# Strassen-like weight sums made by GpSimd in a tile, one addition moved ahead, preparation spread: a streaming encoder layer on one Trainium2 core

## The chip, the cores and the metric

The kernel runs on one core of one Trainium2 chip. The metric is the device time of one execution in microseconds; the median of three runs is compared. Engines are named as in the profile: PE (TensorE), DVE (VectorE), ACT (ScalarE), POOL (GpSimd), SP (SyncE, whose queue issues most of the DMAs).

## The reference

One layer of a streaming encoder on 2048 prompt tokens and 64 sample tokens, all in float32. The part that matters here is the gated MLP at the end of the layer:

```python
h2 = rmsnorm(x, g2) * (1 + sc2) + sh2
up = h2 @ w_up                                   # (T, 1024) @ (1024, 2 * 2816)
upp = jnp.concatenate([conv_buf.astype(up.dtype), up], 1)
conv = b_conv + sum(w_conv[j] * upp[:, j:j + T] for j in range(CONV_W))     # causal, width 3
a, g = jnp.split(conv, 2, -1)
x = x + gt2 * ((jax.nn.silu(g) * a) @ w_down)    # (T, 2816) @ (2816, 1024)
```

Before it come a normalisation, one input projection, a pooling mixer and an mLSTM with four heads, and an output projection; after it a final normalisation. None of these is touched.

## The kernel before, in words

The first 800 us are the attention-like half of the layer, in four groups of tokens. Then the MLP runs over three groups of 704 tokens (o.g = 0, 1, 2). Every float32 operand is split into a high and a low half, and a product is made of three passes (high x high, high x low, low x high). The split of a weight unit is made on the way: a DMA loads the raw weights, ACT copies them to the high half (L385), DVE subtracts to get the low half (L388). `pump` loads ahead and splits; up to six split units are held at a time.

The up projection takes two rows of 128 outputs at a time, row f of `a` and row f of `g`, with two halves of 352 tokens each, as a 2x2 block product of seven products instead of eight. One such unit is a *Pair*. Its products, each of 12 matmuls of 352 columns (L1547), run in this order: B11, B21, T4 of the pair before, T2, T3, B22, T1. The sums of activations (T1 to T4) are made for a whole group ahead of time (`prepare`, `sums_of`, `reload`), the sums of up weights (`wsum`, and split ones in `wsplit`) in the first half of the kernel. Results are in PSUM banks: b1 takes B11, then T2 and T1 on top; b4 takes B21 and is then started afresh by B22; b3 takes T3, and T4 on top. The values are put together on DVE: `ea` (first half-row of `a`, L1609) is B21 in b4 plus a copy `s1` of B11; `eg` (L1555) and the second halves add copies `u2` and `u4` to banks. Then come the convolution: a scale on ACT (L1530) and two taps on DVE (L1535), for `ta` and `tg`, a silu on ACT (L1656), and the gate on DVE. Since these steps lag behind, `Pair.products` weaves those of the old pair in between the products of the new one with `rest(...)`.

The rows f go in parts: 0-4, 5-9, 10-15, 16-21 in groups 0 and 1; 0-5, 6-9, 10-13, 14-17, 18-21 in group 2. After each part the down projection of these rows runs (L2043) and its result is added to x (L2060). In group 2 four of the five down projections are also done by seven products instead of eight (`Quad`, `quad_down`, L1796). They need four sums of down weights for each quad, S1 to S4, held in DRAM in `dsum`. `down_sums` makes these during groups 0 and 1: a copy from DRAM to DRAM by SP's queue (L1778), then an accumulating DMA by POOL's queue (L1781), eight such steps for each of 16 blocks.

Work that is not urgent is kept in six lists of generators (`bg`), and `tick(i)` takes one step of list i at fixed places in the program. List 0 has the final normalisation of the group before, list 1 `prepare` for the next group and then `reload`, list 5 `down_sums`. PE, DVE, ACT and POOL run in the order in which the program is written; SP's order is made by a scheduler, except where `keep_in_program_order` pins a DMA.

Of the kernel before, what the change touches and what calls it, by code (L numbers as in the profile page):

```python
# [9 lines left out]
F32 = mybir.dt.float32  # L10
F32R = mybir.dt.float32r
AF = mybir.ActivationFunctionType
ALU = mybir.AluOpType
# [3 lines left out]
P = 128  # L17
# [17 lines left out]
NP = 8  # L35
S3D, S1D, S2D, S4D = range(4)
EPS = 1e-6
# [26 lines left out]
def tile_layer(ctx: ExitStack, tc: tile.TileContext, xT, vecs, cst, rst, rowv, w_mod, w_ada, w_qkou, w_v, w_pool,  # L64
# [248 lines left out]

    dsum = dr.tile([4, P, 4, NP * P], F32, tag="dsum", name="dsum")

    def quad_units(m, j):

        c = slice(j * 256, j * 256 + 256)
        return [(w_down[2 * m, :, j * 512:(j + 1) * 512], 512), (dsum[m][:, S3D:S1D + 1, c], 512),
                (dsum[m][:, S2D:S4D + 1, c], 512), (w_quad[3, m, :, c], 256)]  # L320

# [1220 lines left out]
    def product(ps, Bo, nm, first):  # L1542
        pump()
        U = get_unit()
        for kc in range(4):
            for pi, (a, b) in enumerate(PASSES):
                pe.matmul(ps[:, :FH], U[:, a, kc * P:(kc + 1) * P], Bo.at(nm, kc, b),  # L1547
                          start=(first and kc == 0 and pi == 0), stop=(kc == 3 and pi == 2), skip_group_check=not first)
            if kc % 2:
                tick(0)  # L1550
        live[0] -= 1

# [7 lines left out]
    class Pair:  # L1560
# [10 lines left out]
        def products(self, old):  # L1571
# [23 lines left out]
            product(b2, Bo, "B21", True)  # L1595
            tick(5)
            rest((old, Pair.scale_a), (older, Pair.split_lo))
            extra(1)
            if old:
                old.last_product()  # L1600
            rest((old, Pair.taps_a), (old, Pair.sum_g0))
            extra(2)
# [3 lines left out]
            rest((old, Pair.scale_g))  # L1606
            self.ea = ext_tile(o, f, "a")
            for (a, b, d) in spans(o, 0):
                dve.tensor_tensor(out=self.ea[:, d:d + b - a], in0=b2[:, a:b], in1=self.s1[:, a:b], op=ALU.add)  # L1609
            self.b3 = mm_ps()  # L1610
# [3 lines left out]
            extra(4)  # L1614
            tick(1)
            product(self.b4, Bo, "B22", True)
            rest((old, Pair.silu))
            extra(5)
            tick(5)
            product(b1, Bo, "T1", False)  # L1620
            tick(5)

# [148 lines left out]
    def down_sums():  # L1771

        for j in range(NP // 2):
            c = slice(j * 256, j * 256 + 256)
            for s, start, more in ((S1D, 2, 3), (S3D, 0, 2), (S2D, S1D, 0), (S4D, S2D, 1)):
                for m in range(4):
                    src = w_quad[start, m, :, c] if s < S2D else dsum[m][:, start, c]
                    tc.keep_in_program_order(nc.sync.dma_start(out=dsum[m][:, s, c], in_=src))  # L1778
                    yield
                for m in range(4):  # L1780
                    pool.dma_start(out=dsum[m][:, s, c], in_=w_quad[more, m, :, c], accum_op=ALU.add)  # L1781
                    yield

    def quad_down(o, j, two, Y, first, midway):

        for m in range(4):
# [4 lines left out]
            def product(ps, u, i, nm, start, on=False):  # L1791
                U = W.at(u)
                for k, quad in enumerate(two):
                    w = (2 * k + i) * P if u == 0 else k * P if u == 3 else (2 * i + k) * P
                    for pi, (x, z) in enumerate(PASSES):
                        pe.matmul(ps, U[:, x, w:w + P], quad.d[nm][z], start=(start and k == 0 and pi == 0),  # L1796
                                  stop=(k == 1 and pi == 2), skip_group_check=not start)
# [160 lines left out]
    bg[5].append(down_sums())  # L1958
    for o in fgroups:
        Bo = B[o.g]  # L1960
        quads, more, held = {}, [], []
        Y = None
        for pi, (f0, f1_) in enumerate(SPARTS if o.g in SGS else PARTS):
# [74 lines left out]
            def down(ps, W, ks, secs, stays=False):  # L2038
                for k in ks:
# [8 lines left out]
                    if todo:  # L2048
                        do()
                    else:  # L2050
                        tick(1 - k % 2)

# [143 lines left out]
```

## Time and profile before

| | before |
|---|---|
| time, median of 3 runs | 2205.1 us (2204.74 to 2205.94) |
| profiled execution, time | 2210.41 us |
| its span, first to last instruction | 2208.6 us |
| mean granted TensorE clock | 0.998 |
| PE busy | 2176.4 us (99%), 13708 matmuls |
| DVE busy | 1626.1 us (74%) |
| ACT busy | 1037.4 us (47%) |
| POOL busy | 276.9 us (13%) |

A row of a group says what an instruction writes and reads by the names in the program, then how many there are, their busy time together and the mean of one, then how long the engine stood idle just before them and for whom. A row in order of time begins with its start and its duration in us; in brackets stand the idle time before it and who ended it. The ends of matmuls are modelled: a 352-column matmul is shown with 321 ns, though the next one starts before that.

### The profile page before, as it was taken

To read this page: it belongs to the slowest core of one execution; us is meant where nothing else is said; L and a number is where in the kernel's file an instruction comes from. 1 tells how busy PE (TensorE), PEld (TensorE's weight loads), DVE (VectorE), ACT (ScalarE), POOL (GpSimd) and SP (SyncE) were. 2 spreads that over 40 slices of the span, in tenths; PEclk is the share of its full clock that TensorE was granted. 3 is DMA by queue.
4 is the path that set the end of the run, shared out by engine and by line. 5 is a ranking of instruction groups with operands and counts; after the bars stand their busy time and mean duration, and the time that the engine had idled before them with its cause. 6 is when DMAs were issued, how large, how long until landed. Compare 5 with 4: busy or idle time off the path is not lost. (4 is left out here: it accounts for less than half of the span.)

```text
span 2208.6 us, 38414 instructions
## 1 busy us (share of the span) xinstructions
PE 2176.4 (99%) x13708; PEld 2064.1 (93%) x13708; DVE 1626.1 (74%) x2996; ACT 1037.4 (47%) x2023; POOL 276.9 (13%) x546
## 2 busy tenths in 40 slices
PE   8999999999999999999999999999999999999998
PEld 7888888888899999999999999999999999999998
DVE  4887659577765768786958677776757597888894
ACT  3653335234243446464626444545435356554554
POOL 0010001001000101010202220101101321121122
PEclk9999999999999999999999999999999999999999
DMA  9978987997898687677858977767569665555552
GB/s 345 358 249 258 333 282 236 326 322 245 291 324 270 214 298 239 224 232 239 236 166 239 308 234 222 222 213 204 176 180 270 194 200 174 162 156 178 156 195 81
DMA packets 304192, 521.68 MB, mean 236 GB/s; under 512 B 27480, under 2 KB 131288, under 8 KB 304000
## 3 DMA queue, kind: packets, MB, share of 16 engines
q1 hardware_dynamic: 283008, 482.74, 66.8%
q10 hardware_dynamic: 11776, 28.09, 3.4%
q0 software_dynamic: 9216, 8.39, 3.1%
q8 instruction: 108, 1.77, 0.3%
q14 instruction: 84, 0.69, 0.1%
HBM read 408.36 MB, written 127.52 MB: 243 GB/s over the span
## 5 line engine op out<-in xcount | busy, mean ns | idle before, releaser
L1547 PE MATMUL mm<-hx,wt 128*128 128x352 f32 x5544 | 889.6, 321 | 10.0 <-DVE ea L1609 8.0
L1547 PEld LDWEIGHTS mm<-hx,wt 128*128 128x128 f32 x5544 | 879.5, 188 | 15.0 <-ACT wt L385 9.4
L442 PE MATMUL mm<-hl,wt 128*128 128x512 f32 (+2 forms) x1920 | 395.8, 358 | 1.4 <-DMA wt<-hl_kept 1.3
L2043 PE MATMUL mm<-av,wt 128*128 128x352 f32 (+2 forms) x2400 | 385.6, 321 | 1.6 <-ACT av L1682 0.9
L385 ACT ACTIVATE wt<-raw 128x512 fp32r<-128x512 f32 (+3 forms) x510 | 288.7, 579 | 205.5 <-PE mm L2043 64.6
L2043 PEld LDWEIGHTS mm<-av,wt 128*128 128x128 f32 x2400 | 380.7, 188 | 3.9 <-ACT av L1682 1.2
L388 DVE TENSOR_TENSOR wt<-raw,wt 128x512 fp32r<-128x512 f32 (+3 forms) x510 | 323.3, 648 | 73.6 <-ACT wt L385 71.3
L442 PEld LDWEIGHTS mm<-hl,wt 128*128 128x128 f32 x1920 | 312.7, 188 | 49.0 <-issue 2.8
L442 PE MATMUL mm<-mx,wt 128*128 128x512 f32 (+1 forms) x960 | 187.0, 354 | 0.3
L442 PEld LDWEIGHTS mm<-mx,wt 128*128 128x128 f32 x960 | 158.8, 188 | 25.8 <-ACT mx L1403 1.1
L385 ACT ACTIVATE wt<-wt 128x512 fp32r<-128x512 f32 x176 | 110.4, 628 | 123.8 <-DMA wt<-wsum 105.3
L388 DVE TENSOR_TENSOR wt<-wt 128x512 fp32r<-128x512 f32 x176 | 122.2, 694 | 58.9 <-ACT wt L385 58.5
L1535 DVE SCALAR_TENSOR_TENSOR tg<-eg,V,tg 128x704 f32<-128x704 f32 (+1 forms) x132 | 125.7, 952 | 40.9 <-ACT tg L1530 38.4
L2060 DVE SCALAR_TENSOR_TENSOR x<-mm,MOD,x 128x352 f32<-128x352 f32 (+4 forms) x152 | 78.0, 560 | 82.6 <-PE mm L2043 82.6
L1535 DVE SCALAR_TENSOR_TENSOR ta<-ea,V,ta 128x704 f32<-128x704 f32 (+1 forms) x132 | 125.7, 953 | 8.5 <-ACT ta L1530 5.9
L1796 PE MATMUL mm<-av,wt 128*128 128x352 f32 x576 | 94.4, 321 | 0.0
L1796 PEld LDWEIGHTS mm<-av,wt 128*128 128x128 f32 x576 | 91.8, 188 | 0.0
L207 DVE SCALAR_TENSOR_TENSOR acc<-raw,CA,acc 128x512 f32<-128x512 f32 x84 | 60.6, 748 | 30.8 <-DMA raw<-w_ada 30.7
L1656 ACT ACTIVATE tg<-tg 128x704 f32<-128x704 f32 (+1 forms) x66 | 52.3, 793 | 62.6 <-DVE tg L1535 62.6
L1555 DVE TENSOR_TENSOR eg<-mm,u 128x352 f32<-128x352 f32 x154 | 70.2, 468 | 14.8 <-ACT u L1625 10.1
L1605 ACT ACTIVATE u<-mm 128x352 f32<-128x352 f32 x66 | 30.3, 459 | 100.7 <-PE mm L1547 66.8
L1139 PE MATMUL mm<-wt,hl 128*128 128x256 f32 (+1 forms) x576 | 70.9, 282 | 0.0
(327 smaller groups left out, 2296.9 us busy)
## 6 DMA issues: line engine op xcount, KB each, us to landing
wt<-hl_kept SPq DMA_DIRECT2D x108, 512.0 KB, 5.9
raw<-w_up SPq DMA_DIRECT2D x198, 256.0 KB, 3.9
wt<-wsum SPq DMA_DIRECT2D x176, 256.0 KB, 4.8
wt<-wsplit SPq DMA_DIRECT2D x88, 512.0 KB, 4.8
w<-w_up SPq DMA_DIRECT2D x88, 256.0 KB, 5.4
wsum<-w SPq DMA_DIRECT2D x44, 512.0 KB, 6.2
wsplit<-wt SPq DMA_DIRECT2D x44, 512.0 KB, 4.4
raw<-w_down SPq DMA_DIRECT2D x88, 256.0 KB, 3.9
```

Source lines behind the costliest of these rows:

```text
L207: dve.scalar_tensor_tensor(out=acc[s], in0=w, scalar=CA[:, k, s:s + 1], in1=acc[s], op0=ALU.mult, op1=ALU.add)
L385: act.activation(u.w[:, 0, :u.n], u.raw[:, :u.n], AF.Copy)
L388: dve.tensor_tensor(out=u.w[:, 1, :u.n], in0=u.raw[:, :u.n], in1=u.w[:, 0, :u.n].bitcast(F32), op=ALU.subtract)
L442: pe.matmul(ps[bi][:, :hi - lo], U[:, a, k % 4 * P:(k % 4 + 1) * P], mv[k][:, b, lo:hi], start=(at == 0 and pi == 0), stop=(k == order[-1] ...
L1139: pe.matmul(ps[ti][:n, :cols], h[4 * kh + k4][:, b, lo:lo + n], U[:, a, k4 % 2 * cols:(k4 % 2 + 1) * cols], start=(kh == 0 and k4 == 0 and ...
L1535: dve.scalar_tensor_tensor(out=t[:, :E], in0=ext[:, j:j + E], scalar=wc(j, f), in1=t[:, :E], op0=ALU.mult, op1=ALU.add)
L1547: pe.matmul(ps[:, :FH], U[:, a, kc * P:(kc + 1) * P], Bo.at(nm, kc, b), start=(first and kc == 0 and pi == 0), stop=(kc == 3 and pi == 2), ...
L1555: dve.tensor_tensor(out=ext[:, d:d + b - a], in0=ps[:, a:b], in1=u[:, a:b], op=ALU.add)
L1656: act.activation(self.tg[:, :E], self.tg[:, :E], AF.Silu)
L1796: pe.matmul(ps, U[:, x, w:w + P], quad.d[nm][z], start=(start and k == 0 and pi == 0), stop=(k == 1 and pi == 2), skip_group_check=not start)
L2043: pe.matmul(ps[i][:, :hi - lo], U[:, a, k % 4 * P:(k % 4 + 1) * P], av[k](b, lo, hi), start=(k == 0 and (a, b) == PASSES[0]), stop=(k == n ...
L2060: dve.scalar_tensor_tensor(out=x3[n][:, a:b], in0=ps[i][:, a - lo:b - lo], scalar=gt2(n, s), in1=x3[n][:, a:b], op0=ALU.mult, op1=ALU.add)
```

## The change

It does three things.

First, in `Pair.products` the addition that makes the first half of `ea` is issued right after the taps of the old pair's `ta`, ahead of the old pair's `eg` addition (`sum_g0`), the quad steps of slot 2 and the product T2; before it stood behind all of these.

Second, `down_sums` now loads the four 128x128 blocks of a unit into a tile `dq` (256 KB, 32 units), makes the four sums with four additions on POOL in place, and stores the tile to `dsum` (256 KB). The layouts of `dsum` and `w_quad` in DRAM change so that a unit is contiguous in each partition, and `quad_units` and `quad_down` index them accordingly. List 5 must be empty before group 2.

Third, the places of the ticks: list 5 gets one after every product (seven in a pair) instead of three in a pair, and half of those in the down projections of groups 0 and 1; list 1 gets a second one in each pair from f = 5 on in these groups, and a quarter of those in the down projections instead of half.

```diff
-    dsum = dr.tile([4, P, 4, NP * P], F32, tag="dsum", name="dsum")
+    dsum = dr.tile([4, P, NP, 2, 2 * P], F32, tag="dsum", name="dsum")
     def quad_units(m, j):
-        c = slice(j * 256, j * 256 + 256)
-        return [(w_down[2 * m, :, j * 512:(j + 1) * 512], 512), (dsum[m][:, S3D:S1D + 1, c], 512),
-                (dsum[m][:, S2D:S4D + 1, c], 512), (w_quad[3, m, :, c], 256)]
+        k = slice(2 * j, 2 * j + 2)
+        return [(w_down[2 * m, :, j * 512:(j + 1) * 512], 512), (dsum[m][:, k, 1], 512), (dsum[m][:, k, 0], 512),
+                (w_quad[m, :, k, 3], 256)]
...
     def product(ps, Bo, nm, first):
...
+        tick(5)
         live[0] -= 1
...
             product(b2, Bo, "B21", True)
-            tick(5)
             rest((old, Pair.scale_a), (older, Pair.split_lo))
...
-            rest((old, Pair.taps_a), (old, Pair.sum_g0))
+            rest((old, Pair.taps_a))
+            self.ea = ext_tile(o, f, "a")
+            for (a, b, d) in spans(o, 0):
+                dve.tensor_tensor(out=self.ea[:, d:d + b - a], in0=b2[:, a:b], in1=self.s1[:, a:b], op=ALU.add)
+            rest((old, Pair.sum_g0))
             extra(2)
             product(b1, Bo, "T2", False)
             self.u2 = half_tile("u2")
             act.activation(self.u2, b1[:, :FH], AF.Copy)
             rest((old, Pair.scale_g))
-            self.ea = ext_tile(o, f, "a")
-            for (a, b, d) in spans(o, 0):
-                dve.tensor_tensor(out=self.ea[:, d:d + b - a], in0=b2[:, a:b], in1=self.s1[:, a:b], op=ALU.add)
...
             tick(1)
+            if not o.last and f >= PARTS[0][1]:
+                tick(1)
             product(self.b4, Bo, "B22", True)
             rest((old, Pair.silu))
             extra(5)
-            tick(5)
             product(b1, Bo, "T1", False)
-            tick(5)
...
     def down_sums():
-        for j in range(NP // 2):
-            c = slice(j * 256, j * 256 + 256)
-            for s, start, more in ((S1D, 2, 3), (S3D, 0, 2), (S2D, S1D, 0), (S4D, S2D, 1)):
-                for m in range(4):
-                    src = w_quad[start, m, :, c] if s < S2D else dsum[m][:, start, c]
-                    tc.keep_in_program_order(nc.sync.dma_start(out=dsum[m][:, s, c], in_=src))
+        for j in range(NP):
+            for m in range(4):
+                q = f1.tile([P, 4, P], F32, tag="dq", name="dq")
+                tc.keep_in_program_order(nc.sync.dma_start(out=q, in_=w_quad[m, :, j]))
+                for _ in range(4):
                     yield
-                for m in range(4):
-                    pool.dma_start(out=dsum[m][:, s, c], in_=w_quad[more, m, :, c], accum_op=ALU.add)
+                a11, a12, a21, a22 = (q[:, i] for i in range(4))
+                pool.tensor_tensor(out=a22, in0=a21, in1=a22, op=ALU.add)
+                pool.tensor_tensor(out=a21, in0=a11, in1=a21, op=ALU.add)
+                yield
+                pool.tensor_tensor(out=a11, in0=a22, in1=a11, op=ALU.add)
+                pool.tensor_tensor(out=a12, in0=a11, in1=a12, op=ALU.add)
+                yield
+                yield
+                tc.keep_in_program_order(nc.sync.dma_start(out=dsum[m][:, j], in_=q.rearrange("p (a b) c -> p a (b c)", a=2)))
+                for _ in range(3):
                     yield
...
     for o in fgroups:
+        if o.g in SGS:
+            drain(5)
...
                     if todo:
                         do()
+                    elif o.last:
+                        tick(1 - k % 2)
                     else:
-                        tick(1 - k % 2)
+                        tick((1, 5, 0, 5)[k % 4])
```

DVE in the third pair of group 1, before; `ta` and `tg` are the convolutions of the old pair, L388 makes the low half of a weight unit (here B22's), L1893 is the final normalisation of group 0:

```order
L1535 SCALAR_TENSOR_TENSOR ta_14315<-ea_14199,V_105,ta_14315 128x704 x2
L1555 TENSOR_TENSOR eg_14288<-mm_14202,u2_14194 128x352
L388 TENSOR_TENSOR wt_14273<-wt_14273 128x512
L1893 SCALAR_TENSOR_TENSOR x4_9283<-x4_9283,V_105,rb_14052 128x352 x2
L1609 TENSOR_TENSOR ea_14361<-mm_14268,s1_14292 128x352
L1535 SCALAR_TENSOR_TENSOR tg_14359<-eg_14288,V_105,tg_14359 128x704 x2
```

The same place in the changed kernel, in which the lines have moved by a few (L1603 is `ea`, L387 the low half, L1900 the final normalisation):

```order
L1534 SCALAR_TENSOR_TENSOR ta_14405<-ea_14266,V_105,ta_14405 128x704 x2
L1603 TENSOR_TENSOR ea_14428<-mm_14359,s1_14383 128x352
L1555 TENSOR_TENSOR eg_14379<-mm_14293,u2_14288 128x352
L387 TENSOR_TENSOR wt_14364<-wt_14364 128x512
L1900 SCALAR_TENSOR_TENSOR x4_9288<-x4_9288,V_105,rb_14141 128x352 x2
L1534 SCALAR_TENSOR_TENSOR tg_14454<-eg_14379,V_105,tg_14454 128x704 x2
```

The addition of `ea` has gone past `eg`, the low half of B22's weights and two steps of the final normalisation; the rest stands as it did.

POOL in the first pairs of group 0, before; `ea`, `eg` and `UC` are the copies of the two columns that a group hands to the next:

```order
L1513 COPY ea<-UC 128x2
L1781 DMA dsum<-w_quad 128x256 x2
L1513 COPY eg<-UC 128x2
L1781 DMA dsum<-w_quad 128x256
L1527 COPY UC<-ea 128x2
L1527 COPY UC<-eg 128x2
```

The same engine there in the changed kernel:

```order
L1512 COPY eg<-UC 128x2
L1780 TENSOR_TENSOR dq<-dq 128x128
L1781 TENSOR_TENSOR dq<-dq 128x128
L1526 COPY UC<-ea 128x2
L1783 TENSOR_TENSOR dq<-dq 128x128
L1784 TENSOR_TENSOR dq<-dq 128x128
L1512 COPY ea<-UC 128x2
L1526 COPY UC<-eg 128x2
```

Where POOL issued DMAs between its small copies, it now makes additions in its own tile, two at a time, and the copy behind them waits for them.

SP at the start of group 0 in the changed kernel, from the load of the first tile `dq` to that of the second:

```order
L1776 DMA dq<-w_quad 128x512
L616 DMA x2d<-scr 128x576
L1869 DMA x_8978<-x2d 128x704 x2
L1869 DMA x_9131<-x2d 128x704
L376 DMA wt<-wsum 128x512
...
L1787 DMA dsum<-dq 128x512
L392 DMA wsplit<-wt 128x1024
L1869 DMA x_9288<-x2d 128x704 x2
L1869 DMA x_9456<-x2d 128x704
L392 DMA wsplit<-wt 128x1024
L376 DMA wt<-wsum 128x512
L1776 DMA dq<-w_quad 128x512
```

The store and the next load of the one tile stand in the same queue as the weight loads (`wt<-wsum`, L376), where before there were copies from DRAM to DRAM.

More of the change, by code (lines that the diff above doesn't have):

```diff
@@ L35 @@
 NP = 8
-S3D, S1D, S2D, S4D = range(4)
 EPS = 1e-6
@@ L1793, in product @@
                 for k, quad in enumerate(two):
-                    w = (2 * k + i) * P if u == 0 else k * P if u == 3 else (2 * i + k) * P
+                    w = k * P if u == 3 else (2 * k + i) * P
                     for pi, (x, z) in enumerate(PASSES):
@@ L2168 @@
         "w_quad": blocks(i["w_down"][0], NF)[:, :, :2 * NP * P].reshape(4, 2, P, NP, 2, P).transpose(
-            1, 4, 0, 2, 3, 5).reshape(4, 4, P, NP * P),
+            0, 2, 3, 1, 4, 5).reshape(4, P, NP, 4, P),
         "st_C": np.concatenate([i["state_mlstm_C"][0, 0].transpose(2, 0, 1),
```

## Prediction

> **What bounds the kernel now.** I read the page first, then who PE waited for, then the order of time on DVE, ACT and SP at each place where PE stood.
>
> ```profile
> span 2208.6 us, 38414 instructions
> PE 2176.4 (99%) x13708; PEld 2064.1 (93%) x13708; DVE 1626.1 (74%) x2996; ACT 1037.4 (47%) x2023; POOL 276.9 (13%) x546
> PEclk9999999999999999999999999999999999999999
> ...
> PE mm L1547 <- DVE ea L1609: 8.0, 10, 1.3
> PE mm L1547 <- ACT wt L385: 1.1, 2, 0.6
> PE mm L2043 <- ACT av L1682: 0.9, 1, 0.9
> ...
> 1826.52 23.75 PE mm L1796 x150
> ```
>
> PE is busy for 99% of the span at full clock, and the change leaves its 13708 matmuls as they are, so only idle time of PE can be won. It is 32.2 us in all, most of it before the first matmul and after the last. From 800 us on, the waits of PE (line: total in us, times, longest) have one large entry: ten waits for the addition `ea` on DVE, L1609. The chain's row gives the beat, 23.75 / 150 = 158 ns for a 352-column matmul. The groups model a matmul's end at 321 ns, so each listed wait is 0.16 us shorter than what PE really lost: 8.0 + 10 x 0.16 = 9.6 us. That is the stock this change can draw on.
>
> Why PE waits there: the product B22 starts afresh in the bank from which `ea` reads B21, so it cannot start before `ea` has read it. DVE works in order, and `ea` stands behind other work. Three places, one of each kind (start, us, what, idle before and its releaser), the first in group 1:
>
> ```profile
> 1304.96 1.94 DVE L1535 SCALAR_TENSOR_TENSOR ta<-ea,V,ta 128x704 f32<-128x704 f32 x2
> 1306.81 0.52 DVE L1555 TENSOR_TENSOR eg<-mm,u 128x352 f32<-128x352 f32 x1
> 1307.25 0.68 DVE L388 TENSOR_TENSOR wt<-wt 128x512 fp32r<-128x512 f32 x1
> 1307.85 1.08 DVE L1893 SCALAR_TENSOR_TENSOR x<-x,V,rb 128x352 f32<-128x352 f32 x2
> 1308.84 0.52 DVE L1609 TENSOR_TENSOR ea<-mm,s 128x352 f32<-128x352 f32 x1
> ...
> 1303.71 4.91 PE L1547 MATMUL mm<-hx,wt 128*128 128x352 f32 x30
> 1309.51 1.19 PE L1547 MATMUL mm<-hx,wt 128*128 128x352 f32 x6 [0.88 <-DVE ea L1609]
> ```
>
> PE restarts 0.15 us after `ea` ends (1309.36 to 1309.51); without it B22 would have begun at about 1308.5.
>
> ```profile
> 1050.53 1.94 DVE L1535 SCALAR_TENSOR_TENSOR ta<-ea,V,ta 128x704 f32<-128x704 f32 x2 [0.24 <-ACT ta L1530]
> 1052.39 0.52 DVE L1555 TENSOR_TENSOR eg<-mm,u 128x352 f32<-128x352 f32 x1
> 1052.82 0.68 DVE L388 TENSOR_TENSOR wt<-wt 128x512 fp32r<-128x512 f32 x1
> 1053.42 0.52 DVE L1609 TENSOR_TENSOR ea<-mm,s 128x352 f32<-128x352 f32 x1
> 1054.09 1.22 PE L1547 MATMUL mm<-hx,wt 128*128 128x352 f32 x6 [0.96 <-DVE ea L1609]
> ...
> 1024.33 1.17 ACT L385 ACTIVATE wt<-wt 128x512 fp32r<-128x512 f32 x2 [4.25 <-DMA wt<-wsum]
> 1024.99 0.69 DVE L388 TENSOR_TENSOR wt<-wt 128x512 fp32r<-128x512 f32 x1 [5.58 <-ACT wt L385]
> 1025.60 0.52 DVE L1609 TENSOR_TENSOR ea<-mm,s 128x352 f32<-128x352 f32 x1
> 1026.26 1.99 PE L1547 MATMUL mm<-hx,wt 128*128 128x352 f32 x11 [0.98 <-DVE ea L1609]
> ...
> SPq L843 <- DMA Bd<-fscr: 5.5, 3, 2.6
> ...
> 1936.21 0.96 DVE L1703 TENSOR_TENSOR fscr<-ta,tg 128x640 f32<-128x640 f32 x2 [0.86 <-ACT tg L1656]
> 1938.79 1.40 PE L1547 MATMUL mm<-hx,wt 128*128 128x352 f32 x7 [0.71 <-DVE ea L1609]
> ```
>
> **Part one, `ea` ahead of the old pair's `eg`.** No instruction is added. `ea` moves ahead of the old row's addition L1555, of the quad steps of slot 2, of the subtraction L388 that makes the low half of B22's own weights, and of what the ticks of T2 put in (here L1893). What stays in the way is that L388: B22's third matmul needs the low half, and it now stands 0.44 us later (the step from L1555 to L388 in the rows above). So each wait becomes the later of two ends.
>
> First kind, more than these stood ahead of `ea`: at 1308 L388 would end at 1307.93 + 0.44 = 1308.4, in time, and all of 0.88 + 0.16 is won. At 1938 `ea` slips into the 0.86 us in which DVE waits for the silu on ACT. Four of the ten are of this kind (1309.5, 1791.1, 1938.8, 2019.7); taking off what L388 still holds back in three of them I take 3.5 us of their 3.9. Second kind, nothing but L1555 and L388 stood between (1054.1, 1549.6, 2100.1, 2142.5): DVE finishes both at the same moment as before, only in another order, and B22 gains the two matmuls that run before the low half is needed, 2 x 0.158 = 0.32 us; four of them 1.3 us. Third kind, a late load holds L388 itself (1026.3, 1495.8): PE starts at the weights' end, 1025.68, rather than behind `ea`, and the third matmul runs at 1025.8 where it ran at 1026.6; 0.8 us each, 1.6. Four shorter stops (841, 1776, 1858, 2127), listed under ACT or too short to be listed, also end 0.15 us after an `ea`; by the same reading 1.5 us. Sum 7.9 us won, with ends 4.5 (fourteen places of the second kind, 14 x 0.32) and 11 (the 9.6 and those 1.5, all of it).
>
> What is late next: the old `eg` starts 0.44 us later where DVE is behind, and with it the copy `u` on ACT, which waits for `eg` to have read the old one, and the weight splits queued behind that copy. `u` is wanted by T1, two products after T2; B22's 12 x 158 ns = 1.9 us cover it. I take nothing; without the cover 0.44 us at some of the fourteen places.
>
> **Part two, the sums for the down product made on POOL.** It takes out 64 additions by DMA from POOL's queue and 64 copies from SP's, and adds 32 loads and 32 stores of 256 KB on SP and 128 additions of 128x128 on POOL.
>
> ```profile
> L1781 POOL DMA_DIRECT2D dsum<-w_quad x64 | 53.3, 897 | 13.9 <-issue 11.4 <-DMA wsplit<-wt 1.1 <-DMA dsum<-w_quad 0.8
> L1953 POOL TENSOR_TENSOR ssum<-ssum,fscr 128x704 f32<-128x704 f32 x16 | 28.5, 1781 | 86.4 <-ACT fscr L1952 86.1
> L1937 POOL TENSOR_TENSOR y<-x,fscr 128x256 f32<-128x256 f32 x3 | 2.1, 726 | 1.3 <-ACT fscr L1920 1.3
> ...
> dsum<-w_quad SPq DMA_DIRECT2D x32, 128.0 KB, 5.2
> dsum<-dsum SPq DMA_DIRECT2D x32, 128.0 KB, 4.2
> ```
>
> An addition of 128 columns: (1781 - 726) / 448 = 2.35 ns a column, 726 - 128 x 2.35 = 0.43 us; 128 of them 55 us, as much as the 53.3 us of DMA issues that go. Bytes and SP issues stay level (64 for 64). POOL's other work in these stages is copies of two columns, on which nothing of PE waits. So POOL itself costs nothing. What is new is that POOL reads and writes SBUF beside DVE:
>
> ```profile
> 1251.43 1.71 POOL L1953 TENSOR_TENSOR ssum<-ssum,fscr 128x704 f32<-128x704 f32 x1 [2.59 <-ACT fscr L1952]
> 1251.84 1.84 DVE L388 TENSOR_TENSOR wt<-raw,wt 128x512 fp32r<-128x512 f32 x1 [1.04 <-ACT wt L385]
> ...
> L388 DVE TENSOR_TENSOR wt<-wt 128x512 fp32r<-128x512 f32 x176 | 122.2, 694 | 58.9 <-ACT wt L385 58.5
> ```
>
> L388, 0.69 us elsewhere, took 1.84 us: it stood until POOL was done at 1253.14. So a unit of four additions can hold DVE up to 4 x 0.43 = 1.72 us. By the ticks the 32 units lie in groups 0 and 1 up to about 1500 us, roughly 24 in pair stages, about one to each of 33 pairs. DVE has room there on average (windows of group 0's pair stages; the third time is DVE's):
>
> ```profile
> 804.60:873.00 68.40, 67.11 (x426) 66.00 (x426) 53.27 (x85) 40.93 (x70) 13.21 (x26) 1.00 0.89 284
> 913.00:977.60 64.60, 64.60 (x410) 64.60 (x409) 53.20 (x84) 39.39 (x70) 8.88 (x22) 1.00 0.82 251
> 1017.50:1098.60 81.10, 79.16 (x495) 78.31 (x494) 64.77 (x99) 47.32 (x82) 15.86 (x28) 1.00 0.80 239
> 1146.00:1224.00 78.00, 78.00 (x495) 78.00 (x494) 59.53 (x90) 43.69 (x75) 12.53 (x27) 1.00 0.81 240
> ```
>
> Idle is 15.1 + 11.4 + 16.3 + 18.5 = 61 us against at most 22 x 1.72 = 38 us. Only additions that fall between the taps and B22, some 4 us of a pair's 13.3, reach PE: 24 x 0.3 x 1.72 = 12 us of delay on DVE, most of it inside the spare that nearly all pairs have (PE stands in 10 of 66). I take 1.5 us, near the end at nothing, since waits of DVE for ACT such as the 0.24 us above take up part; the ends are 0 and 12.
>
> The Trainium skill, SBUF — State Buffer, Who interferes with whom, says that a DVE instruction with two SBUF inputs contends with a GpSimd one that reads SBUF, and that whichever issued first makes the other wait. The rows above agree for POOL first. By that rule a DVE that is never idle would make POOL pay instead, this term would be 0 and the sum 7.9 us of gain (an estimate).
>
> **Part three, preparation spread.** The next group's preparation gets a second tick in most pairs and half as many in the down stages; its instructions stay. It moves some 0.5 to 1 us of DVE work into a pair, behind the taps of `tg`, where DVE has idle time. The reload of sums waits in the same list. SP's waits for buffers of the preparation (L843, 5.5 us in three) delayed loads before; slower steps should ease that, and may move it. I take 0, ends -1 and +2.
>
> **Sum.** -7.9 + 1.5 + 0 = -6.4 us. The profiled execution took 2210.4 us with a span of 2208.6, 5.3 us above the median of the runs, 2205.1, to which I apply it: 2198.7 us.
>
> **Rivals.**
> *The wait changes its name.* In all places DVE owes B22 both L388 and `ea`, and the low half ends as late as `ea` did. Speaks for it the second place; against it the first, with 1.08 us in between. Then 14 x 0.32 = 4.5 us less 1.5: 2202.1.
> *POOL holds up DVE, slower.* Place: L388 and the taps just ahead of B22 in groups 0 and 1. For it the 1.84 us row; against it the 61 us idle. If all 12 us reach PE and the additions run into one another as two of L1953's do, so that half of the 38 us counts, 19 - 7.9 = 11: 2216. It decides from 12.3 us of lost DVE time in the windows before B22.
> *SP held by the single `dq` tile.* The next load waits for the store, the store for POOL, and weight loads stand behind both. The third kind above shows what a late load costs, 0.4 to 1 us. Five of 64 would bring 4: 2202.7, no change to tell.
>
> **Chances.** Forecast 0.64 (this range alone 2196 to 2200.6); wait renamed 0.17; SP 0.09; POOL 0.10. A difference under 0.2%, 4.4 us, is about what a measurement of this kernel can't tell from none: faster 0.64, same 0.26, slower 0.10. The range 2195 to 2206 leaves out the slow rival and a gain beyond 10 us.
>
> **What would show it.** PE's wait for `ea` falls from 8.0 us to under 1 and a wait for L388's successor of 2 to 4 us appears, the largest near 2142. POOL shows four groups of 32 additions near 0.43 us. The mean of 694 ns of the `wt<-wt` subtraction rises in groups 0 and 1 alone. Group 2, in which POOL adds nothing, should gain about 4 us by itself. I am wrong if PE idles more in groups 0 and 1 than before, or if B22 still waits for `ea`.

## The result: 2217.8 us, slower by 0.56%

| | before | after |
|---|---|---|
| median on the same chip | 2204.9 us (4 runs, 2204.2 to 2205.9) | 2217.8 us (4 runs, 2213.8 to 2219.9) |
| ratio | | 1.0056 (1.0038 to 1.0073) |
| profiled execution | 2210.4 us | 2218.3 us |

The forecast was 2198.7 us, and 2217.8 lies outside its range. The page of after and the waits of PE from 800 us on (line: total in us, times, longest):

```profile
span 2216.5 us, 38327 instructions
PE 2181.4 (98%) x13708; PEld 2067.2 (93%) x13708; DVE 1640.8 (74%) x2996; ACT 1037.1 (47%) x2023; POOL 293.4 (13%) x610
...
PE mm L1546 <- DVE wt L387: 10.4, 16, 1.4
PE mm L1546 <- DVE eg L1555: 1.9, 3, 1.2
...
PE mm L1546 <- DVE ea L1603: 0.2, 1, 0.2
```

The wait for `ea` is gone, from 8.0 us to 0.2. In its place stands a wait for L387, the low half of a weight unit, that is larger than the one removed. Where it lies is told by the length of the stages, from the first product matmul of a part to the first matmul of its down projection, and from there to the first product of the next part (worked out from the starts of the matmuls; T4 of a part's last pair runs inside the down projection and counts there; "before, again" is a second profile of the same kernel, below):

| stage, us | before | before, again | after |
|---|---|---|---|
| group 0, pairs 5 to 9 | 64.6 | 64.6 | 69.1 |
| the down projection behind them | 39.9 | 40.0 | 42.4 |
| group 1, pairs 0 to 4 | 68.6 | 68.9 | 70.3 |
| group 1, pairs 5 to 9 | 64.6 | 64.6 | 67.6 |
| the down projection behind them | 39.9 | 39.9 | 40.7 |
| group 1, pairs 10 to 15 | 79.9 | 78.7 | 77.9 |
| group 2, all pairs | 292.4 | 292.4 | 290.3 |
| whole MLP, first product to last | 1347.5 | 1345.1 | 1356.5 |

The loss is in slots 5 to 9 and the down projection behind them, some 10.7 us in the two groups, where the pairs have a second preparation tick and most of the preparation runs. One of these places in order of time (start, us, what, idle before and its releaser): PE at the third matmul of B11 of slot 8, DVE and ACT ahead of it:

```profile
951.84 1.85 PE L1546 MATMUL mm<-hx,wt 128*128 128x352 f32 x10 [0.82 <-DVE wt L387]
...
947.74 2.15 DVE L1534 SCALAR_TENSOR_TENSOR tg<-eg,V,tg 128x704 f32<-128x704 f32 x2
949.81 0.94 DVE L725 SCALAR_TENSOR_TENSOR fscr<-fscr,G,rb 128x704 f32<-128x704 f32 x1
950.67 0.51 DVE L775 TENSOR_TENSOR fscr<-fscr 128x352 f32<-128x352 f32 x1
951.11 0.68 DVE L387 TENSOR_TENSOR wt<-raw,wt 128x512 fp32r<-128x512 f32 x1
952.60 0.69 DVE L387 TENSOR_TENSOR wt<-raw,wt 128x512 fp32r<-128x512 f32 x1 [0.82 <-ACT wt L384]
...
947.60 0.62 ACT L384 ACTIVATE wt<-raw 128x512 fp32r<-128x512 f32 x1
950.78 0.88 ACT L727 ACTIVATE fscr<-fscr,MOD 128x704 f32<-128x704 f32 x1 [2.56 <-DVE fscr L725]
951.57 0.48 ACT L765 ACTIVATE fscr<-fscr 128x352 fp32r<-128x352 f32 x1
951.96 0.61 ACT L384 ACTIVATE wt<-raw 128x512 fp32r<-128x512 f32 x1
952.48 0.78 ACT L1656 ACTIVATE tg<-tg 128x704 f32<-128x704 f32 x1
```

L725 and L775 are two steps of the preparation. They stand on DVE between the taps of `tg` and the low half that PE wants, and end the wait 1.3 us later than it would have ended. ACT is hit more: L727, the second half of the first step, reads what DVE makes behind the taps, and ACT stands 2.56 us for it, with the next weights' high half (951.96) and the silu (L1656) in line behind. So the low half after that (952.60) is late too. The Trainium skill, Perfetto Trace Analysis, Tensor Engine Instruction (MATMUL, LD_WEIGHTS), says that ACT, DVE and GPSIMD are strict first-in-first-out queues; these rows agree for ACT and DVE.

Two of the four POOL groups of the new sums, and the low halves of `wt<-wt` (x count, busy, mean ns):

```profile
L1784 POOL TENSOR_TENSOR dq<-dq 128x128 f32<-128x128 f32 x32 | 22.9, 716 | 2.5
...
L1781 POOL TENSOR_TENSOR dq<-dq 128x128 f32<-128x128 f32 x32 | 20.6, 643 | 2.5
...
L387 DVE TENSOR_TENSOR wt<-wt 128x512 fp32r<-128x512 f32 x176 | 123.2, 706 | 36.0 <-ACT wt L384 35.7
```

With the other two (531 and 678 ns) an addition takes 0.64 us in the mean, not the 0.43 us worked out before, and 82 us in all.

### The profile page after: what moved, and what is told of

Same layout as the page of the kernel before. It is cut to its first block, busy times and chain, and to the rows that moved or that the text cites. A ratio compares the mean times of both kernels' runs of the same rounds, so it can differ in the third digit from the quotient of the medians.

```text
span 2216.5 us, 38327 instructions
## 1 busy us (share of the span) xinstructions
PE 2181.4 (98%) x13708; PEld 2067.2 (93%) x13708; DVE 1640.8 (74%) x2996; ACT 1037.1 (47%) x2023; POOL 293.4 (13%) x610
## 3 DMA queue, kind: packets, MB, share of 16 engines
q1 hardware_dynamic: 285056, 491.13, 67.6%
## 4 chain that ended last, share of the span: by engine, by line
PE 84%; DVE 5%; DMA 5%; ACT 2%; issue 2%; SPq 1%; POOL 0%; DVEq 0%; ACTq 0%; POOLq 0%
PE mm L1546 31%; PE mm L441 23%; PE mm L2052 16%; PE mm L1803 5%; PE mm L1138 3%; DMA wt<-wsum 2%; DVE wt L387 1%; DVE tg L1534 1%; PE m L1319 1%; PE m L1320 1%; DVE ta L1534 1%; PE m L1308 1%; PE m L1297 1%; DMA raw<-w_ada 1%; ACT wt L384 1%
## 5 line engine op out<-in xcount | busy, mean ns | idle before, releaser
L1546 PE MATMUL mm<-hx,wt 128*128 128x352 f32 x5544 | 895.3, 322 | 12.8 <-DVE wt L387 10.4
L387 DVE TENSOR_TENSOR wt<-raw,wt 128x512 fp32r<-128x512 f32 (+3 forms) x510 | 326.6, 653 | 78.4 <-ACT wt L384 77.0
L387 DVE TENSOR_TENSOR wt<-wt 128x512 fp32r<-128x512 f32 x176 | 123.2, 706 | 36.0 <-ACT wt L384 35.7
L2071 DVE SCALAR_TENSOR_TENSOR x<-mm,MOD,x 128x352 f32<-128x352 f32 (+4 forms) x152 | 77.9, 559 | 85.3 <-PE mm L2052 85.2
L1656 ACT ACTIVATE tg<-tg 128x704 f32<-128x704 f32 (+1 forms) x66 | 52.2, 791 | 59.8 <-DVE tg L1534 59.8
L1337 POOL TENSOR_TENSOR sf<-sf,half 128x4 f32<-128x4 f32 (+1 forms) x20 | 21.3, 1066 | 380.1 <-DVE sf L1335 328.6
```

Of the source, the lines that this page charges most:

```text
L387: dve.tensor_tensor(out=u.w[:, 1, :u.n], in0=u.raw[:, :u.n], in1=u.w[:, 0, :u.n].bitcast(F32), op=ALU.subtract)
L1656: act.activation(self.tg[:, :E], self.tg[:, :E], AF.Silu)
L2071: dve.scalar_tensor_tensor(out=x3[n][:, a:b], in0=ps[i][:, a - lo:b - lo], scalar=gt2(n, s), in1=x3[n][:, a:b], op0=ALU.mult, op1=ALU.add)
```

## The experiments

Each was timed in turns with the kernel before, on one chip; the ratio is to that kernel, with its 95% interval. The chip is not the same for all, so ratios are compared here rather than medians.

| kernel | median, us | ratio |
|---|---|---|
| `e_only`: the move of `ea` alone | 2204.6 | 0.9995 (0.9986 to 1.0004) |
| `e_p`: move and POOL's sums | 2206.0 | 1.0004 (0.9995 to 1.0013) |
| `e_s`: move and spread | 2218.2 | 1.0059 (1.0046 to 1.0071) |
| `e_s_noadd`: after without POOL's additions | 2213.3 | 1.0033 (1.0021 to 1.0046) |
| `pair2`: `e_p` and the second tick in pairs | 2213.2 | 1.0034 (1.0022 to 1.0047) |
| `down_half`: `e_p` and the halved ticks in down projections | 2209.2 | 1.0013 (1.0004 to 1.0023) |
| `after_lo`: after, one low half ahead of the ticks | 2214.4 | 1.0038 (1.0025 to 1.0051) |
| `after_split`: after, ACT's half of a step one tick later | 2215.9 | 1.0045 (1.0033 to 1.0057) |
| `after_late`: after, both ticks behind the silu | 2211.9 | 1.0027 (1.0014 to 1.0039) |
| `pair2_late`: `pair2`, both ticks behind the silu | 2209.3 | 1.0018 (1.0009 to 1.0027) |
| `pair2_apart`: one of them behind T1 | 2208.4 | 1.0007 (0.9998 to 1.0016) |
| `lo_first`: `e_only`, B22's low half ahead of `eg` | 2212.7 | 1.0032 (1.0020 to 1.0045) |
| `e_late`: `e_only`, its one tick behind the silu | 2204.1 | 0.9995 (0.9985 to 1.0004) |
| `e_down`: `e_only`, all ticks in down projections | 2257.1 | 1.0233 (1.0220 to 1.0246) |
| `best`: `e_late`, and `lo_first` in group 2 alone | 2201.8 | 0.9978 (0.9967 to 0.9988) |
| `best_p`: `best` and POOL's sums | 2203.7 | 0.9991 (0.9982 to 1.0000) |

**Which of the three parts loses the time.** At first I held the second tick to be the cause (theory one), against POOL's additions (theory two).

```diff
 # e_only, from before                            # e_s: e_only and
+rest((old, Pair.taps_a)); self.ea = ...          +if not o.last and f >= PARTS[0][1]: tick(1)
+rest((old, Pair.sum_g0))                         # and in down: tick(1), nothing, tick(0), nothing
 # e_p: after without the second tick, down as before (tick(1 - k % 2)) and its tick(5) beside
 # e_s_noadd: after without the four pool.tensor_tensor
```

> Only the first half-row's addition moved; sums by DMA and the preparation's ticks as in the kernel before. Both theories: faster. The changed kernel gained 2.2 us in group 2, where neither POOL's additions nor the preparation run, and the kernel before lost 5.6 us at B22 in groups 0 and 1; about half of that should come back too, since L388 then stands at the same places. Expected 2200 us (2197 to 2202). At 2205 the move is worth nothing, and the forecast's first term falls with it.

> The move and POOL's sums, without the spread of the preparation. Theory one (the second tick puts 1 to 2.4 us of preparation on DVE between the taps of tg and the low half that the next product needs): the time of the move alone, within 2 us of it, about 2201. Theory two (POOL's additions, 0.64 us each where I had 0.43, hold DVE up): most of the loss stays, 2212 or more.

> The move and the spread of the preparation, with the sums still made by DMA. Theory one: most of the loss is there, 2211 to 2216, and the pairs of slots 5 to 9 in groups 0 and 1 are 3 us longer each group than before. Theory two: about 2200, as the move alone.

> The changed kernel with the 128 additions on POOL left out (its loads and stores stay; what is stored are then not the sums). Theory one: as the move and the spread together, 2211 to 2216. Theory two: the loss is gone, 2200 to 2203. If the two add up, halfway, near 2209.

The move and POOL's sums together make no difference that can be told (1.0004); the move and the spread are as slow as the change (1.0059 against 1.0056). So the spread costs about 0.5 to 0.6%, 11 to 14 us. Theory one holds on this, but the move alone gave 1 us where I expected 5. The fourth kernel came out between: with the spread in place, leaving POOL's additions out gives 5 us back (1.0033 against 1.0056, with overlapping intervals). That is not the price of POOL's additions against sums by DMA: `e_s` makes the sums by DMA, adds nothing on POOL, and is as slow as the change (1.0059). With the spread in place the two ways of making the sums can't be told apart; `e_s_noadd` is the kernel that makes none at all, and why that one is faster stays open.

How little work the spread moves is seen in slots 5 to 9 of group 0 (window, its length, busy time of PE, PEld, DVE, ACT, POOL, clock, DMA share, GB/s); the second row of each pair counts DVE's work on the preparation's tiles `fscr` alone. First `e_p`, then after:

```profile
911.00:975.60 64.60, 64.60 (x410) 64.60 (x409) 54.71 (x85) 40.32 (x71) 14.07 (x28) 1.00 0.78 256
911.00:975.60 64.60, 4.28 (x9) 1.00 0.78 256
```

```profile
911.40:980.50 69.10, 66.70 (x410) 65.02 (x409) 55.31 (x83) 38.10 (x67) 14.38 (x28) 1.00 0.75 250
911.40:980.50 69.10, 5.08 (x10) 1.00 0.75 250
```

One DVE instruction more, 0.8 us in five pairs, and the stage is 4.5 us longer, with DVE idle for 14 us of it. DVE is not short of time. What differs is where the steps stand and whom they wait for. The waits of ACT in the same two windows, first `e_p`, then after, of which the rows with `fscr` are the preparation's:

```profile
ACT wt L384 <- DMA wt<-wsum: 7.7, 8, 1.7
...
ACT fscr L765 <- DVE fscr L781: 1.9, 1, 1.9
...
ACT fscr L727 <- DVE fscr L725: 0.7, 1, 0.7
```

```profile
ACT wt L384 <- DMA wt<-wsum: 15.5, 9, 4.6
ACT fscr L727 <- DVE fscr L725: 4.9, 2, 2.6
ACT u L1608 <- DVE eg L1555: 3.4, 2, 2.0
...
ACT fscr L765 <- DVE fscr L781: 2.4, 1, 2.4
```

ACT stands 7.3 us for the preparation instead of 2.6. Its longest wait, for loads of weights (`wt<-wsum`), doubles too, from 7.7 us to 15.5, which would speak for late loads as the cause. But in `after_late` below it is 16.0 us, and the stage takes 65.3 us: that wait alone does not lengthen the stage.

**Pairs or down projections, and order or load.**

```diff
 # pair2: e_p                     # down_half: after            # after_lo
+if not o.last and f >= ...:     -if not o.last and f >= ...:    extra(4)
+    tick(1)                     -    tick(1)                   +pump()
                                                                 tick(1)
 # lo_first: e_only, and pump() behind the addition of ea, ahead of sum_g0
```

> The changed kernel with its down stages' ticks as before: of the spread only the second tick in the pairs from slot 5 on is left. Theory A (the second tick's DVE work stands ahead of the low half that the third matmul of the next B11 needs): most of the 12 us that the spread costs is here, 2212 to 2217, with stops at the third matmul of B11 in slots 5 to 9. Theory B (fewer ticks in the down stages leave the preparation late, and its last steps fall where DVE has no room): about 2206, as the kernel with the move and POOL's sums alone.

> The changed kernel without the second tick in the pairs; the down stages give the preparation half as many ticks. Theory A: about 2206. Theory B: 2212 or more. The preparation then ends some pairs later, and each pair has one step as before.

> The changed kernel with one line more: the weights' splits that the pairs' B22 would make first are made before the preparation's ticks rather than behind them, so that the low half for the next B11 stands ahead of both steps. Theory A (order on DVE): most of the 12 us come back, 2205 to 2209. If DVE is short of time altogether in those pairs, or the loads come late, the order changes nothing: 2215 to 2219.

> The kernel before with the first half-row's addition moved, and the low half of B22's weights moved ahead of the old row's addition and of the steps of slot 2 too. In the run with the addition alone moved PE stood 8.0 us in products, 4.4 of them at B22's third matmul, for that low half. If the order on DVE is all, those go: 2200 to 2202. If the low half is held by ACT or by a load, nothing more: 2204 to 2205.

The second tick costs 0.30% against `e_p` (6.6 us). The halved ticks cost 0.09% (2 us), which the intervals don't separate from nothing; but the down projection behind slots 5 to 9 of group 0 takes 42.1 us there and 39.9 in `e_p`. With both 0.52% go. `after_lo` gives a third of the loss back, with an interval that overlaps that of the change, and is nearer to the time named for "the order changes nothing" than to the other: most stops at B11 go, but its waits for L387 (4.5 us) are joined by 6.3 us for `eg`, which now stands behind. `lo_first` is the plainest miss. B22's stop goes, and B11 of the next pair stops instead. Slots 3 and 4 of group 2, PE and DVE:

```profile
1799.73 1.07 PE L1547 MATMUL mm<-hx,wt 128*128 128x352 f32 x5 [1.03 <-DVE wt L388]
...
1793.44 0.53 DVE L1604 TENSOR_TENSOR ea<-mm,s 128x352 f32<-128x352 f32 x1
1793.88 0.68 DVE L388 TENSOR_TENSOR wt<-wt 128x512 fp32r<-128x512 f32 x1
1794.48 0.52 DVE L1555 TENSOR_TENSOR eg<-mm,u 128x352 f32<-128x352 f32 x1
...
1797.14 1.94 DVE L1535 SCALAR_TENSOR_TENSOR tg<-eg,V,tg 128x706 f32<-128x706 f32 x2
1798.99 1.29 DVE L388 TENSOR_TENSOR wt<-raw,wt 128x512 fp32r<-128x512 f32 x2
```

From 1783.8 to 1800.2 DVE has no gap that the view marks. In this stretch, where DVE has a backlog, the other order only chose which product stops. In groups 0 and 1 the same order made slots 5 to 9 of group 0 longer by 3.4 us and slots 10 to 15 of group 1 by 3.1 us against `e_only`; I did not pursue through which instruction. In slots 18 to 21 of group 2 it shortened the stage from 53.9 us to 52.6.

**Place, wait or amount.** A tick behind the silu leaves the weights' splits and the silu ahead of the preparation.

```diff
 # after_late, e_late              # after_split, in prepare: act.activation(x, ..., bias=sh2) of L727
     extra(4)                      #   is issued at the next tick, ahead of that one's DVE step
-    tick(1)                       # e_down: no tick(1) in pairs of groups 0, 1;
     product(self.b4, Bo, "B22")   #   in down: tick(1) twice, then tick(0) and tick(1)
     rest((old, Pair.silu))
     extra(5)
+    tick(1)
```

> The changed kernel with both of a pair's preparation ticks moved from between the taps of tg and B22 to behind the old row's silu and ahead of T1; the number of ticks, and all work, stay. Theory P (place: two steps on DVE and ACT stand ahead of the splits of the next B11's and B21's weights and of the silu): those stops go, 2204 to 2208. Theory Q (amount: DVE and ACT have no room for a second step in a pair wherever it stands): 2214 to 2219.

> The changed kernel with the normalization's two halves in steps of their own: ACT's L727 is issued a tick later than the DVE operation L725 that it reads, so that ACT, which runs in order, no longer stands for it with the weights' splits and the silu queued behind. ACT stood 26 us for L725 in the changed kernel, up to 2.6 us at a time. If that wait carries the loss (theory A-wait): 2207 to 2211. If it is DVE's own two steps ahead of the low half: 2214 to 2219.

> The kernel before with the first half-row's addition moved, and its single tick in a pair moved behind the silu, ahead of T1. Theory P: the stops at the third matmul of B11 go (1.7 us in four in the run with the addition alone moved): 2202 to 2204. Theory Q: no change, 2204 to 2206.

> The opposite of the spread: the kernel before with the addition moved, no preparation tick in the pairs of groups 0 and 1, and twice as many in their down stages, where DVE is idle for a fifth to two fifths of the time. Both theories: the pairs' stops in groups 0 and 1 go. 2201 to 2203, if the down stages take the steps; if the preparation isn't done by the end of the group, its rest is drained in one piece and the time is above 2206.

`after_late` gives half of the loss back; its 2211.9 us lies between the ranges of the two theories. Slots 5 to 9 take 65.3 us and 64.6 us in groups 0 and 1, where after took 69.1 and 67.6, and ACT's waits for the preparation in that stage of group 0 are back at 2.3 us:

```profile
913.70:979.00 65.30, 65.30 (x410) 64.54 (x409) 54.06 (x82) 38.94 (x68) 16.31 (x28) 1.00 0.79 258
...
ACT wt L384 <- DMA wt<-wsum: 16.0, 8, 5.0
...
ACT fscr L727 <- DVE fscr L725: 1.6, 2, 0.9
...
ACT fscr L765 <- DVE fscr L781: 0.7, 1, 0.7
```

So the place of the ticks, theory P, accounts for most of the loss in the pairs, though not for all of it: `pair2_late` below has the ticks at the same place, and there that stage takes 67.1 us in group 0 and 64.6 in group 1. The later place also moves the last steps out of the stage: it holds 8 instructions of the preparation on DVE and not 10, and together with the down projection it takes 107.7 us, where after took 111.5 and `e_p` 104.6. What stays here is in the down projections behind the pairs, 42.4 us as in after. T4 of slot 9 waits there for the old `eg`:

```profile
983.90 1.35 PE L1546 MATMUL mm<-hx,wt 128*128 128x352 f32 x7 [1.83 <-DVE eg L1555]
...
981.76 0.69 DVE L387 TENSOR_TENSOR wt<-raw,wt 128x512 fp32r<-128x512 f32 x1 [0.98 <-ACT wt L384]
...
983.24 0.52 DVE L1555 TENSOR_TENSOR eg<-mm,u 128x352 f32<-128x352 f32 x1
...
980.71 0.50 ACT L765 ACTIVATE fscr<-fscr 128x352 fp32r<-128x352 f32 x1 [1.22 <-DMA Bd<-fscr]
981.11 0.62 ACT L384 ACTIVATE wt<-raw 128x512 fp32r<-128x512 f32 x1
```

Here ACT stands for a store of the preparation (`Bd<-fscr`), the split of a weight stands behind it, and `eg` behind that split. `after_split` is unclear: 0.11% less than after, with overlapping intervals. With two ticks at one place a tick later is the same moment: in that stage ACT still stood 1.9 us for L725, and 2.4 us for another step. `e_late` is no faster than `e_only` (both 0.9995), though the stops at B11's third matmul went down to two.

`e_down` shows another wait. Where the kernel before gives the preparation one tick in its down projections, this one gives it three (not two, as expected), and now the step's own load isn't there (DVE, and PE's stop behind it):

```profile
901.94 0.95 DVE L726 SCALAR_TENSOR_TENSOR fscr<-fscr,G,rb 128x704 f32<-128x704 f32 x1 [3.00 <-DMA fscr<-x2d]
...
922.44 0.95 DVE L726 SCALAR_TENSOR_TENSOR fscr<-fscr,G,rb 128x704 f32<-128x704 f32 x1 [3.18 <-DMA raw<-w_up]
...
925.22 0.68 DVE L388 TENSOR_TENSOR wt<-raw,wt 128x512 fp32r<-128x512 f32 x1
...
925.96 6.36 PE L1547 MATMUL mm<-hx,wt 128*128 128x352 f32 x22 [6.21 <-DVE wt L388]
```

(At 922.44 the trace names a weight load that landed last; the step is the same.) I had expected 2201 to 2203 since DVE is idle there for a fifth to two fifths of the time; it took 2257.1. Not all of these 52 us are stops: the granted clock of PE, 1.00 in `e_only` from 904 to 945 us, was 0.83 here from 904 to 925 and 0.75 from 925 to 945. Over the whole profile it was 0.988 against 0.999, which would be up to 25 us (an estimate, 0.011 of 2255). The empty `yield`s in `prepare` are waiting time: ticks are its clock, and here a step that came early made the engine, and all behind it, wait for a load (the rows above), a store or the other engine. That the rest would be drained in one piece is not what happened: the preparation was over before slot 10.

**The stock, and what is left.**

> The kernel before, unchanged, for a second profile. The first profiled execution took 5.3 us more than the median. If the ten waits of 8.0 us for ea were partly that execution's own (above all the two behind a late load, at 1026 and 1495), they are now fewer: 5 to 6 us in all, and the MLP's stops 9 us or less. If they are the kernel's, 8 us and 12.5 us again, and the 7.9 us were lost only because the waits moved on.

> The kernel before with the first half-row's addition moved, for a second profile. Its first had 8.0 us of stops in products, at ten places for L388 or ea. If the stops are set by the order on DVE and ACT, the places at 1.2 us in group 2 are there again; those of groups 0 and 1 come and go by a load's arrival.

> The move, POOL's sums and the second tick in the pairs, both ticks behind the silu, the down stages' ticks as before: the changed kernel with both halves of the spread's loss mended as I understand them. If the place of the ticks in the pair (7 us of loss) and the halved ticks of the down stages (3 to 5 us) are all of it: within 2 us of the kernel with the move and POOL's sums alone, 2204 to 2208. If a second step in a pair costs wherever it is: 2210 or more.

> The move, the single tick behind the silu, and in the last group alone the low half of B22's weights ahead of the old row's addition. In the last group that order shortened the slots 18 to 21 by 1.3 us against the move alone, and the others by 0.4 us; in groups 0 and 1 it cost 7 us and is left as it was. Expected 2202 to 2203 against 2204.1 for the same kernel without it. If the wait only moves to the next B11, 2204.

The kernel before a second time (2207.1 us), its waits of PE for `ea` and for the high halves:

```profile
PE mm L1547 <- DVE ea L1609: 5.0, 7, 1.3
PE mm L1547 <- ACT wt L385: 2.3, 4, 0.9
```

The six stops of 0.4 us and more in group 2 are there again, five within 0.01 us and one 0.15 us shorter; the two behind a late load, at 1026 and 1495, are not. All stops over 0.15 us in products are 12.5 us in the first profile and 10.5 in the second; with the move 8.0 (`e_only`) and 6.8 (`e_again`), where again the stops of group 2 repeat and those of groups 0 and 1 come and go. So each explanation had a part: the stock was 2 us smaller than counted, and what remained was won only partly.

`pair2_late` gives back some 4 us of `pair2`'s loss and ends 0.14%, 3 us, above `e_p`: between the 2 us that I expected to be left at most and the 2210 us or more of the other case, with overlapping intervals. `best` is faster than both kernels: 0.22% (0.12 to 0.33) below before. Against `e_late`, without the order of group 2, it is 0.17% (3.7 us), but the intervals overlap, and the stages of group 2 show 1.0 us of it. Its waits of PE:

```profile
PE mm L1547 <- DVE wt L388: 2.4, 3, 1.1
...
PE mm L1547 <- DVE eg L1555: 0.8, 2, 0.5
```

> As the kernel with both ticks behind the silu and the down stages as before (2209.3), but the second tick moved behind T1, a product later, so that two steps of the preparation no longer follow one another directly. Theory S (a step needs time after the one before: its store, its other engine's half): ACT stands less for the preparation in slots 5 to 9 of group 0 (5.6 us there before), and the time is 2205 to 2207. Theory Q (a second step costs wherever it is): 2208 to 2211.

> The fastest kernel so far (2201.8: move, tick behind the silu, low half first in the last group) with POOL's sums in place of the sums by DMA. If POOL's additions cost 1 to 2 us, as they did with the move alone: 2203 to 2204; if they cost nothing: 2201 to 2202.

With the second tick behind T1, the kernel is level with `e_p` by its ratio (1.0007 against 1.0004), which speaks for theory S; its median, 2208.4 us, lies in the range of theory Q, and its interval overlaps that of `pair2_late`. ACT stands less for the preparation in slots 5 to 9 of group 0, as theory S has it (3.2 us, all for `Bd<-fscr`, against 5.6), but the stage is no shorter: 67.7 us against 67.1. So the spacing is not shown to be worth anything. POOL's sums cost 0.13% on `best`, as 0.09% on `e_only`: that is 2 to 3 us, and neither can be told from nothing: the intervals overlap.

## Why the prediction was wrong

*The step that failed: preparation spread, "I take 0, ends -1 and +2".* It measured 11 to 14 us. I priced the step by DVE's busy time, "some 0.5 to 1 us of DVE work into a pair", and covered it with DVE's idle time. The busy time was even less than that (0.8 us more in all five pairs of slots 5 to 9 of group 0), and the idle time was there. What I left out is the queue: which instructions stand behind the step on DVE and on ACT, and that the step's ACT half waits for its DVE half behind two taps. The row that could have told it stood in the trace of before, in the groups of ACT between 800 and 1720 us:

```profile
L728 ACT ACTIVATE fscr<-fscr,MOD 128x704 f32<-128x704 f32 (+2 forms) x24 | 15.5, 683 | 20.5 <-DVE fscr L726 20.4
```

ACT stood 20.4 us for 24 of these steps, 0.85 us for each. I looked at SP's waits for the preparation's buffers alone and hoped that slower steps would ease them. That the place in the queue is the cause is shown for the half of the loss that `after_late` gives back with the same number of ticks; for the rest, in the down projections and at the later place, it is argued from single places.

*The term of the move, -7.9 us, was far too large.* The move alone gave 1.1 us (a loss of 0.9 to a gain of 3.1); in the profiles, two of each kernel, its stops are some 4 us fewer and its MLP is some 2 us shorter. The mechanism was as told: `ea` is ready, and PE next waits for the low half. But the stock came from one execution that took 5.3 us more than the median, which I had noted and not used; its two stops of the third kind were gone in the second profile. And I credited the places of the first kind with nearly all of their wait. Two of the four, 1938 and 2019, were won in full. At 1791 the low half held PE for 1.34 us where `ea` had held it for 1.07, because a quad step stands ahead of it, and at 1309 0.63 of the 1.05 us won went to new stops at T4 and the next B11. The place of 2142.5 was of another kind than I put it in: after the move, between `ea` and the low half there still stands a 1.07 us step of the quads. Rows of `e_only`, the same place:

```profile
2134.36 0.53 DVE L1604 TENSOR_TENSOR ea<-mm,s 128x352 f32<-128x352 f32 x1
2134.80 0.52 DVE L1555 TENSOR_TENSOR eg<-mm,u 128x352 f32<-128x352 f32 x1
2135.23 1.07 DVE L1844 SCALAR_TENSOR_TENSOR x<-x,MOD,fscr 128x640 f32<-128x640 f32 x2
2136.22 0.69 DVE L388 TENSOR_TENSOR wt<-wt 128x512 fp32r<-128x512 f32 x1
...
2136.96 1.23 PE L1547 MATMUL mm<-hx,wt 128*128 128x352 f32 x6 [1.09 <-DVE wt L388]
```

So the rival in which the wait changes its name was the nearer one for this part; even its 4.5 us was too much. Group 2 gained some 2 us by its stages, not 4.

*POOL's term, +1.5 us, is not contradicted:* 2 to 3 us by the ratios, and a cost of zero lies within the intervals too. Its parts were off in both directions. The additions take 0.64 us and not 0.43. DVE's busy time over the whole span rises from 1628.3 us in `e_only` to 1638.2 in `e_p`, by 9.9 us, where I had allowed at most 38 us and put 12 us of it just ahead of B22. That half of a rival, *POOL holds up DVE*, gives nearly the measured time (2216) is chance: its place, L388 and the taps in groups 0 and 1, is where the loss lies, but its cause is not. The mean of the `wt<-wt` subtraction rose from 694 to 706 ns only. With the spread in place POOL's sums cost nothing that can be told either (`after` against `e_s`).

*The single `dq` tile* had no case: SP's next load stood 22.7 us in all for the store of that tile in after, and as long in `e_p` (21.8), which is no slower than the kernel before.

Of what should show it: the wait for `ea` fell below 1 us as told; the wait for L387 was 10.4 us in sixteen places and not 2 to 4, seven of the ten longest of them at the third matmul of B11, a product that the prediction never looked at. That PE would idle more in groups 0 and 1 was named as the sign of being wrong, and is what happened.

One thing stays open. By the stages the profiled MLP of after is 9.0 us longer than the first of before and 11.4 us longer than the second, and the stops over 0.15 us in its products are 4.0 and 6.0 us more (16.5 against 12.5 and 10.5). Nearly all of the rest lies in delays below that bound: product matmuls that start between 7 ns and 0.15 us later than the beat of 158 ns add up to 8.2 us in after and to 3.3 and 4.1 us in the two profiles of before. About half of the 8.2 us is made of stretches in which a matmul starts every 167 ns, as from 1312 to 1319 us, at a granted clock of 1.00 (499 matmuls, against 100 and 169); what makes them is not known.

## What to carry to other kernels

Price a step of background work that is woven into a pipeline by what stands behind it in each queue that it enters, not by its busy time against an engine's idle share: here 0.8 us of work cost a stage 4.5 us, and half of the change's loss came back by moving the same steps a few instructions down, behind the silu. A generator that is driven by ticks has its waits for loads, stores and other engines built into the spacing of the ticks; changing their rate or place changes what each step finds ready. And before a stock of waits is counted as a gain, profile the kernel twice: here five of the six larger waits of group 2, set by the order, came again to 0.01 us, and the two behind a late load did not come again.

## What I had not expected of the hardware

A POOL addition of 128 columns of float32 took 0.53 to 0.72 us in the mean of its group, where the additions of 256 and 704 columns before lead to 0.43. The length goes with DVE's work: in after the 19 additions that ran mostly while DVE was idle took 0.46 us in the mean, the 109 others 0.67, and the longest 1.2. DVE pays as well: its busy time is 1637.9 to 1640.8 us in the profiles of all kernels with the additions and 1625.5 to 1628.9 in all those without. Of these 10 us or so the kernel's time shows 2 to 3, and even those within the intervals. The Trainium skill, Perfetto Trace Analysis, GPSIMD Engine Instruction, says to take a GPSIMD instruction's span as unreliable and to go by the spacing of starts; in one unit of after (at 946 us) the additions of L1781, L1783 and L1784 start 1.05 and 0.87 us apart with spans of 0.98 and 0.79 us, and in all 84 places of after where one addition follows another at once the spacing is 0.08 us more than the span, so here the spans can be used.
